# HGRN recurrence: eight heads written out as one pipeline in a fixed order, with an eighth of the reciprocals

## The chip, the cores and the metric

The kernel runs on one core of one Trainium2 chip. The metric is the device time of one execution in microseconds (us); lower is better. Times shown for the kernel before are three runs and one profiled execution.

## The reference, cut to what matters

The kernel computes two transformer-like blocks on a 512 x 1024 input. The change touches one part of the first block: the bidirectional HGRN2 scan over 8 heads, each with 128 key and 128 value channels, on 512 latent tokens after 256 context tokens.

```python
def _hgrn_scan(q, k, v, logf, S):      # S_t = diag(f_t) S_{t-1} + k_t v_t^T, o_t = S_t^T q_t
    L = H_CHUNK
    ...
        b = jnp.cumsum(lf, axis=2)
        attn = jnp.einsum('bhtd,bhtsd,bhsd->bhts', qc, decay, kc)
        o = jnp.einsum('bhtd,bhdv->bhtv', qc * jnp.exp(b), S) + jnp.einsum('bhts,bhsv->bhtv', attn, vc)
        S_new = jnp.exp(b_last)[..., None] * S + jnp.einsum('bhsd,bhsv->bhdv', kc * jnp.exp(b_last[:, :, None, :] - b), vc)
    ...
def _hgrn_gates(f_pre, lb):
    logf = jnp.log(lb + (1.0 - lb) * jax.nn.sigmoid(fp))
    k = (1.0 - lb) * jax.nn.sigmoid(-fp)
```

It is run once forwards and once backwards in time, and the two outputs are added. Gates f, keys k and queries q come from projections of the normed input by 1024 x 128 weight blocks, one block per head for q, for the forward gate and for the backward gate.

## The kernel before

The program is written in a tile framework: the source emits instructions for TensorE (PE), VectorE (DVE), ScalarE (ACT) and GpSimd (POOL), and a scheduler that plays the program through in advance chooses the order in which each engine's queue gets them. Buffers have tags with a number of slots; an instruction that wants a slot waits until its last user is done.

The stage in question is `block1_hgrn` (L981 on). Tokens are cut into 64 blocks of 8. For a head, `hgrn_head` makes q from one projection; `hgrn_dir`, called for both directions d, makes the gates F and the keys K from a second (512 latent columns) and a third (256 context columns) projection, and from them products of gates inside each block of 8: G (running products outwards from the middle of the block), R, the reciprocals of all 512 elements of G (L840), and the scaled queries Q1 and keys K1. Then `pre` and `suf` hold, for each of four levels, the products over the blocks that lie before and after a block inside a pair, a quad and so on (the loop at L862 to L873, run for each direction), and E holds the decays of the context (a scan, L882 and L885).

Products on TensorE: Y1, Y2 (inside a block, L907), then four levels (L910 to L926) in which both directions are put into one QM and one KM tile and multiplied into the PSUM banks X and Z; transposes of E and of KL (L953, L957), copied by ACT into kt; pk (L961, L963), the state increments, which S (L967, DVE) chains up; and po (L972 to L974), the output.

A projection (`proj`, `mm3`) is 24 matmuls on a weight block split into a high and a low part: `split_w` has ACT write the high part (L203) and DVE the low part (L204). Every weight block takes one such pair. The PSUM tags are `a` (four banks: X, Z, Y1, Y2 of a head, later pk of each direction), `p` (two, projections) and `t` (two, transposes and po). One `hgrn_head` after another is emitted, and the scheduler is free to lay the next head's projections and gates between the products of this one.

Of the kernel before, what the change touches and what calls it, by code (L numbers as in the profile page):

```python
# [8 lines left out]
F32 = mybir.dt.float32  # L9
# [5 lines left out]
ALU = mybir.AluOpType  # L15
# [3 lines left out]
KT = 8  # L19
# [123 lines left out]
class Net:  # L143
# [654 lines left out]
    def hgrn_dir(self, h, d, q):  # L798

        nc, w = self.nc, self.wk  # L800
        j = (self.HFF if d == 0 else self.HFB) + h
        wt = self.mix_w(j)
        F = w.tile([128, TA], F32, tag="w3", bufs=3, name=self.nm("F"))
        K = w.tile([128, TA], F32, tag="w3", bufs=3, name=self.nm("K"))
        bc = j - 4 + 4
        for seg, o, wd in (("x", 0, T), ("c", T, TC)):
            ps = self.proj(wt, seg)
            for t, b, sc in ((F, self.v("b_mix"), 1.0), (K, self.nbm, -1.0)):
                if seg == "x":
                    ov, iv = t[:, :T].rearrange("p (w r) -> p r w", r=8), ps.rearrange("p (r w) -> p r w", r=8)  # L810
                else:
                    ov, iv = t[:, T:], ps
                nc.scalar.activation(ov, iv, AF.Sigmoid, bias=b[:, j : j + 1], scale=sc)  # L813
        c = d * 8 + h
        nc.vector.tensor_scalar(F, F, self.omlb[:, c : c + 1], self.lb[:, c : c + 1], ALU.mult, ALU.add)
        f = F[:, :T].rearrange("p (b e) -> p b e", e=8)
        G = w.tile([128, 64, 9], F32, tag="w9", bufs=1, name=self.nm("G"))

        def two(t, i0, i1):

            st = i1 - i0
            return t[:, :, i0 : (i1 + (1 if st > 0 else -1)) if (st > 0 or i1 > 0) else None : st]

        mu = lambda o, a, b: nc.vector.tensor_tensor(o, a, b, ALU.mult)
        if d == 0:
            mu(two(G, 1, 5), two(f, 2, 4), two(f, 3, 5))
            mu(two(G, 0, 6), two(G, 1, 5), two(f, 1, 6))
            mu(two(G, 7, 8), two(G, 6, 0), two(f, 7, 0))
            nc.vector.tensor_copy(two(G, 2, 4), two(f, 3, 4))
            nc.gpsimd.memset(G[:, :, 3:4], 1.0)  # L830
            tL, tR = G[:, :, 8], G[:, :, 7]
        else:
            mu(two(G, 2, 6), two(f, 2, 4), two(f, 3, 5))
            mu(two(G, 1, 7), two(G, 2, 6), two(f, 1, 6))
            mu(two(G, 0, 8), two(G, 1, 7), two(f, 0, 7))
            nc.vector.tensor_copy(two(G, 3, 5), two(f, 3, 4))
            nc.gpsimd.memset(G[:, :, 4:5], 1.0)
            tL, tR = G[:, :, 0], G[:, :, 8]
        R = w.tile([128, 64, 8], F32, tag="w2", bufs=16, name=self.nm("R"))
        nc.vector.reciprocal(R, G[:, :, 0:8])  # L840
        Q1 = w.tile([128, 64, 8], F32, tag="w2", bufs=16, name=self.nm("Q1"))
        K1 = w.tile([128, 64, 8], F32, tag="w2", bufs=16, name=self.nm("K1"))
        kx = K[:, :T].rearrange("p (b e) -> p b e", e=8)
        qx = q.rearrange("p (b e) -> p b e", e=8)
        lo, hi = slice(0, 4), slice(4, 8)
        qg, qr = (hi, lo) if d == 0 else (lo, hi)
        om = self.omlb[:, c : c + 1]
        nc.vector.scalar_tensor_tensor(Q1[:, :, qg], qx[:, :, qg], om, G[:, :, qg], ALU.mult, ALU.mult)
        nc.vector.scalar_tensor_tensor(Q1[:, :, qr], qx[:, :, qr], om, R[:, :, qr], ALU.mult, ALU.mult)
        nc.gpsimd.tensor_tensor(K1[:, :, qr], kx[:, :, qr], G[:, :, qr], ALU.mult)  # L850
        nc.gpsimd.tensor_tensor(K1[:, :, qg], kx[:, :, qg], R[:, :, qg], ALU.mult)

        pre = w.tile([128, 5, 64], F32, tag="wp", bufs=4, name=self.nm("pre"))
        suf = w.tile([128, 5, 64], F32, tag="wp", bufs=4, name=self.nm("suf"))
        nc.vector.tensor_copy(pre[:, 0], tL)
        nc.vector.tensor_copy(suf[:, 0], tR)
        tots = w.tile([128, 128], F32, tag="wt", name=self.nm("tots"))
        o = 0
        n = 64
        mu(tots[:, 0:64], tL, tR)  # L860
        cur = tots[:, 0:64]
        for lv in range(4):  # L862
            m = 1 << lv
            pv = lambda t, i: t[:, i].rearrange("p (n two m) -> p n two m", two=2, m=m)
            tv = cur.rearrange("p (n two) -> p n two", two=2)
            nn = 64 // (2 * m)
            mu(pv(pre, lv + 1)[:, :, 1], pv(pre, lv)[:, :, 1], tv[:, :, 0:1].broadcast_to([128, nn, m]))
            nc.vector.tensor_copy(pv(pre, lv + 1)[:, :, 0], pv(pre, lv)[:, :, 0])
            mu(pv(suf, lv + 1)[:, :, 0], pv(suf, lv)[:, :, 0], tv[:, :, 1:2].broadcast_to([128, nn, m]))
            nc.vector.tensor_copy(pv(suf, lv + 1)[:, :, 1], pv(suf, lv)[:, :, 1])  # L870
            o += n
            n //= 2
            mu(tots[:, o : o + n], tv[:, :, 0], tv[:, :, 1])  # L873
            cur = tots[:, o : o + n]
        T128 = cur

        Fc, Kc = F[:, T:], K[:, T:]
        E = w.tile([128, TC], F32, tag="w1", bufs=1, name=self.nm("E"))
# [8 lines left out]
        return Q1, K1, pre, suf, T128, E  # L887

    def hgrn_head(self, h, v):
        nc, w = self.nc, self.wk  # L890
        wq = self.mix_w(self.HQ + h)
        ps = self.proj(wq, "x")
        bq = self.v("b_mix")[:, self.HQ + h : self.HQ + h + 1]
        sg = w.tile([128, T], F32, tag="w2", bufs=16, name=self.nm("sg"))
        nc.scalar.activation(sg, ps, AF.Sigmoid, bias=bq)
        q = w.tile([128, T], F32, tag="w2", bufs=16, name=self.nm("q"))
        nc.vector.scalar_tensor_tensor(q.rearrange("p (w r) -> p r w", r=8), ps.rearrange("p (r w) -> p r w", r=8), bq,
                                       sg.rearrange("p (r w) -> p r w", r=8), ALU.add, ALU.mult)
        D2 = [self.hgrn_dir(h, d, q) for d in range(2)]
        bc = lambda a, m: a.unsqueeze(a.ndim if hasattr(a, "ndim") else len(a.shape)).broadcast_to(list(a.shape) + [m])  # L900
        mm = nc.tensor.matmul
        X, Z, Y1, Y2 = [self.bank("a") for _ in range(4)]
        flat = [[D2[d][i].rearrange("p b e -> p (b e)") for i in range(2)] for d in range(2)]
        for Y, (qf, kf) in ((Y1, flat[0]), (Y2, flat[1])):
            for c in range(4):
                cs = slice(c * 128, c * 128 + 128)
                mm(Y[:, cs], kf[:, cs], qf[:, cs], start=True, stop=True)  # L907

        (Qf, Kf, pf, sf, _, _), (Qb, Kb, pb, sb, _, _) = D2
        for lv, dst, hb in ((3, X, 128), (2, X, 64), (1, X, 32), (0, Z, 128)):  # L910
            m = 1 << lv
            bv = lambda t: t.rearrange("p (n two m) e -> p n two m e", two=2, m=m)
            pv = lambda t: t[:, lv].rearrange("p (n two m) -> p n two m", two=2, m=m)
            QM = w.tile([128, 64, 8], F32, tag="w2", bufs=16, name=self.nm("QM"))
            KM = w.tile([128, 64, 8], F32, tag="w2", bufs=16, name=self.nm("KM"))
            for (o, a, p, i, e) in ((QM, Qf, pf, 1, nc.vector), (QM, Qb, sb, 0, nc.vector),
                                    (KM, Kf, sf, 0, nc.gpsimd), (KM, Kb, pb, 1, nc.gpsimd)):
                if m == 1:
                    e.tensor_tensor(bv(o)[:, :, i, 0], bv(a)[:, :, i, 0], bc(pv(p)[:, :, i, 0], 8), ALU.mult)
                else:  # L920
                    e.tensor_tensor(bv(o)[:, :, i], bv(a)[:, :, i], bc(pv(p)[:, :, i], 8), ALU.mult)
            qm, km = QM.rearrange("p b e -> p (b e)"), KM.rearrange("p b e -> p (b e)")
            for c in range(4):
                for b in range(128 // hb):
                    bs = slice(c * 128 + b * hb, c * 128 + b * hb + hb)
                    mm(dst[b * hb : b * hb + hb, bs], km[:, bs], qm[:, bs], start=True, stop=True)  # L926
# [1150 lines left out]
```

## Time and profile before

| what | value |
| --- | --- |
| three runs, median | 2606.16 us (2605.35 to 2611.03) |
| profiled execution, its own time | 2607.22 us |
| span of the profiled execution | 2605.4 us |
| TensorE busy in the span | 2512.9 us (96%) |
| VectorE busy in the span | 1651.4 us (63%) |

Busy time of TensorE is made of modelled ends, so a share of 96% says that its queue was rarely empty and not that it ran at its peak. The shares are means over stages that have different limits; the stage of the change is about 319 us of the span.

### The profile page before, as it was taken

To read this page: it belongs to the slowest core of one execution; us is meant where nothing else is said; L and a number is where in the kernel's file an instruction comes from. 1 tells how busy PE (TensorE), PEld (TensorE's weight loads), DVE (VectorE), ACT (ScalarE), POOL (GpSimd) and SP (SyncE) were. 2 spreads that over 40 slices of the span, in tenths; PEclk is the share of its full clock that TensorE was granted. 3 is DMA by queue.
4 is the path that set the end of the run, shared out by engine and by line. 5 is a ranking of instruction groups with operands and counts; after the bars stand their busy time and mean duration, and the time that the engine had idled before them with its cause. 6 is when DMAs were issued, how large, how long until landed. Compare 5 with 4: busy or idle time off the path is not lost. (4 is left out here: it accounts for less than half of the span.)

```text
span 2605.4 us, 38102 instructions
## 1 busy us (share of the span) xinstructions
PE 2512.9 (96%) x15116; PEld 2157.3 (83%) x15116; DVE 1651.4 (63%) x3087; ACT 965.1 (37%) x1711; POOL 452.2 (17%) x567
## 2 busy tenths in 40 slices
PE   6999999999989998999999999999999899999998
PEld 4888888899988888898888898888886668888887
DVE  8777767746499996324433366665555777766665
ACT  5312211236233332425422363232343556533333
POOL 3000000012043344214000011062013440100001
PEclk8999999999999999999999999999999999999999
DMA  6434664621211111111333342344423223333332
GB/s 230 174 125 145 230 216 178 226 90 66 85 41 50 33 50 41 37 49 41 89 121 97 96 139 89 117 127 154 137 72 112 64 77 99 109 97 96 97 97 72
DMA packets 88307, 277.94 MB, mean 107 GB/s; under 512 B 12912, under 2 KB 31104, under 8 KB 79936
## 3 DMA queue, kind: packets, MB, share of 16 engines
q1 hardware_dynamic: 85344, 265.00, 31.7%
q0 software_dynamic: 2064, 7.35, 0.8%
q10 hardware_dynamic: 720, 3.15, 0.3%
q8 instruction: 119, 1.95, 0.3%
q14 instruction: 60, 0.49, 0.1%
HBM read 262.88 MB, written 12.59 MB: 106 GB/s over the span
## 5 line engine op out<-in xcount | busy, mean ns | idle before, releaser
L204 DVE TENSOR_TENSOR wlo<-wraw,whi 128x1024 fp32r<-128x1024 f32 (+1 forms) x341 | 423.2, 1246 | 235.2 <-ACT whi L203 105.0
L203 ACT ACTIVATE whi<-wraw 128x1024 fp32r<-128x1024 f32 (+1 forms) x341 | 355.4, 1053 | 553.7 <-PE psa L216 158.1
L215 PE MATMUL psp<-xmh,whi 128*128 128x512 f32 (+1 forms) x760 | 281.1, 377 | 3.7 <-ACT K L813 3.1
L216 PE MATMUL psp<-xml,whi 128*128 128x512 f32 (+1 forms) x744 | 272.4, 373 | 0.0
L350 POOL TENSOR_TENSOR ssum<-ssum,sq 128x256 f32<-128x256 f32 x40 | 30.2, 754 | 962.0 <-ACT sq L348 961.5
L215 PE MATMUL psa<-xmh,whi 128*128 128x512 f32 x496 | 194.0, 391 | 0.0
L216 PE MATMUL psa<-xml,whi 128*128 128x512 f32 x496 | 193.9, 391 | 0.0
L215 PE MATMUL psu<-xmh,whi 128*128 128x512 f32 x496 | 193.5, 390 | 0.0
L216 PE MATMUL psu<-xml,whi 128*128 128x512 f32 x496 | 193.3, 390 | 0.0
L215 PE MATMUL pso<-hh,whi 128*128 128x512 f32 (+1 forms) x512 | 184.3, 365 | 1.8 <-DVE hr L496 1.8
L216 PE MATMUL pso<-hl,whi 128*128 128x512 f32 (+1 forms) x512 | 184.2, 365 | 0.0
L215 PEld LDWEIGHTS psp<-xmh,whi 128*128 128x128 f32 x760 | 148.5, 195 | 29.0 <-ACT K L813 4.7
L305 DVE SCALAR_TENSOR_TENSOR ajunk<-araw,crow 128x1024 bf16<-128x1024 f32 x128 | 156.4, 1222 | 25.2 <-DMA araw<-in_ada_r_dram 19.6
L218 PE MATMUL psp<-xmh,wlo 128*128 128x512 f32 (+1 forms) x744 | 170.3, 368 | 0.0
L492 DVE SCALAR_TENSOR_TENSOR xr<-pso,hgate,xr 128x512 f32<-128x512 f32 x128 | 95.3, 749 | 109.8 <-PE pso L218 109.7
L216 PEld LDWEIGHTS psp<-xml,whi 128*128 128x128 f32 x744 | 145.1, 195 | 22.1 <-issue 0.6
L218 PEld LDWEIGHTS psp<-xmh,wlo 128*128 128x128 f32 x744 | 129.3, 189 | 26.3 <-issue 4.4
L218 PE MATMUL pso<-hh,wlo 128*128 128x512 f32 (+1 forms) x512 | 145.2, 365 | 0.0
L218 PE MATMUL psa<-xmh,wlo 128*128 128x512 f32 x496 | 126.8, 389 | 0.0
L218 PE MATMUL psu<-xmh,wlo 128*128 128x512 f32 x496 | 124.0, 390 | 0.0
L215 PEld LDWEIGHTS pso<-hh,whi 128*128 128x128 f32 x512 | 97.2, 190 | 16.5 <-DVE hr L496 2.0
L444 ACT ACTIVATE hh<-sa 128x512 fp32r<-128x512 f32 x66 | 36.7, 560 | 197.1 <-DVE sa L441 197.0
(667 smaller groups left out, 5818.1 us busy)
## 6 DMA issues: line engine op xcount, KB each, us to landing
araw<-in_ada_r_dram SPq DMA_DIRECT2D x52, 1024.0 KB, 5.5
wraw<-in_ffn_in_dram SPq DMA_DIRECT2D x88, 512.0 KB, 4.3
wraw<-in_mix_fm_dram SPq DMA_DIRECT2D x65, 512.0 KB, 3.6
wraw<-in_ffn_out_dram SPq DMA_DIRECT2D x44, 512.0 KB, 3.7
wraw<-in_up_dram SPq DMA_DIRECT2D x44, 512.0 KB, 3.7
wraw<-in_down_dram SPq DMA_DIRECT2D x22, 512.0 KB, 3.7
araw<-in_ada_w_dram SPq DMA_DIRECT2D x8, 1024.0 KB, 11.7
wraw<-in_mix_out_dram SPq DMA_DIRECT2D x14, 512.0 KB, 3.7
```

The lines of the kernel that those rows point to most:

```text
L203: nc.scalar.activation(hi, raw, AF.Copy)
L204: nc.vector.tensor_tensor(lo, raw, hi.bitcast(F32), ALU.subtract)
L215: self.nc.tensor.matmul(ps, wh, xh, start=k == 0, stop=False)
L216: self.nc.tensor.matmul(ps, *((wl, xh) if last else (wh, xl)), start=False, stop=False)
L218: self.nc.tensor.matmul(ps, *((wh, xl) if last else (wl, xh)), start=False, stop=k == n - 1)
L305: nc.vector.scalar_tensor_tensor(junk, w[:, h], 1.0, cr[:, n], ALU.mult, ALU.mult, accum_out=o[:, k : k + 1])
L350: (eng or nc.vector).tensor_tensor(acc, acc, t, ALU.add)
L444: nc.scalar.activation(hh, sa, AF.Copy)
L492: self.anchor = nc.vector.scalar_tensor_tensor(res[n], p, gt[:, n : n + 1], res[n], ALU.mult, ALU.add)
```

## The change

`hgrn_dir` and `hgrn_head` go; `hgrn_pipe` writes all eight heads out inside `tc.manual_schedule(engines={PE, DVE, Activation, Pool})`. Inside that region each of the four engines takes its instructions in the order in which the source emits them; the SP queue (weight loads) and where other stages' instructions fall between stay the scheduler's. Parts:

- gates: the products G go straight into rows of one tile `hgx`, and both a product and its reciprocal partner are laid out so that one reciprocal of 128 elements per direction does, the others following by multiplication with f. Of DVE's three small copies per head and direction, two become ACT copies (one in `hgx`, one into PS0) and one is folded into a product; the scaling of the latent F goes to ACT too.
- block products: one tile holds before/after and both directions, so that a level is one multiplication, one copy and one total for all four.
- order in one turn of the loop for head h, with n = h+1: first projection of n; Q1; levels 3 and 2; Y1, Y2; second projection of n; levels 1 and 0; QL, KL; forward gates of n; transposes; both context projections of n; split of the next weight block; backward gates of n; the copies that free X, Z, Y1, Y2; block products of n; pk; context scan of n; q projection of n; split; S; po; split; output copies.

```diff
+    def hgrn_gates(self, h, d, F, K, PS0):
...
+            nc.scalar.activation(at(q_ + 3, k_ + 5), f(3, 4), AF.Copy)
+            mu(at(q_ + 2, k_ + 6), f(2, 4), f(3, 5))
+            mu(at(q_ + 1, k_ + 7), at(q_ + 2, k_ + 6), f(1, 6))
+            mu(one(q_ + 0), one(q_ + 1), f(0))
+            mu(PS0[:, 1, d], one(k_ + 7), f(7))
+            nc.scalar.activation(PS0[:, 0, d], one(q_ + 0), AF.Copy)
+            nc.vector.reciprocal(at(k_ + 0, q_ + 7), at(q_ + 0, k_ + 7))
...
-        R = w.tile([128, 64, 8], F32, tag="w2", bufs=16, name=self.nm("R"))
-        nc.vector.reciprocal(R, G[:, :, 0:8])
...
+    def hgrn_pipe(self, v):
...
+        for h in range(8):
+            n = h + 1
+            more = n < 8
+            if more:
+                fx = [self.hgrn_fx(n, 0, wt[0])]
+                PS0, K1n = ps0(), []
+            Q1 = self.hgrn_q1(h, *pq)
+            X, Z, Y1, Y2 = [self.bank("a") for _ in range(4)]
+            self.hgrn_level(3, X, 128, Q1, K1, lev)
+            self.hgrn_level(2, X, 64, Q1, K1, lev)
...
+            if more:
+                fx.append(self.hgrn_fx(n, 1, wt[1]))
+            self.hgrn_level(1, X, 32, Q1, K1, lev)
+            self.hgrn_level(0, Z, 128, Q1, K1, lev)
...
+            if more:
+                K1n.append(self.hgrn_gates(n, 0, *fx[0], PS0))
+            kts = []
+            for d in range(2):
...
+                nc.scalar.activation(kt[:, 0:2], pt[:, :256].rearrange("p (c t) -> p c t", c=2), AF.Copy)
...
+            if more:
+                fc = [self.hgrn_fc(n, d, wt[d]) for d in range(2)]
+                wq = wt[2]
+            if n < 7:
+                raw = self.hgrn_w(n + 1)
+                wt = [self.hgrn_split(raw[0])]
+            if more:
+                K1n.append(self.hgrn_gates(n, 1, *fx[1], PS0))
...
+            nc.scalar.activation(at, X, AF.Copy)
+            nc.vector.copy_predicated(v4(at), m4(self.m8), v4(Z))
...
+            T128 = ends
+            if more:
+                lev, ends = self.hgrn_blocks(PS0)
+            pks, S = [], []
+            for d in range(2):
+                pk = self.bank("a", [128, 4, 128])
...
+            if more:
+                E = [self.hgrn_ctx(n, d, *fc[d]) for d in range(2)]
+                pq = self.hgrn_q(n, self.proj(wq, "x"))
+            if n < 7:
+                wt.append(self.hgrn_split(raw[1]))
+            for i in range(3):
+                for d in range(2):
...
+                    nc.vector.scalar_tensor_tensor(S[d][:, i + 1], S[d][:, i], T128[:, 4 * d + c : 4 * d + c + 1], pks[d][:, i + 1],
+                                                   ALU.mult, ALU.add)
+            po = self.bank("o", [128, 4, 128])
...
+            if n < 7:
+                wt.append(self.hgrn_split(raw[2]))
...
+                with tc.manual_schedule(engines={e.PE, e.DVE, e.Activation, e.Pool}):
+                    self.hgrn_pipe(v)
```

## Rows read from the trace of the kernel before

**Rows 1.** Page, busy us of each engine (share of the span) x instructions.
```profile
PE 2512.9 (96%) x15116; PEld 2157.3 (83%) x15116; DVE 1651.4 (63%) x3087; ACT 965.1 (37%) x1711; POOL 452.2 (17%) x567
```

**Rows 2.** Windows: stretch, length, busy us by engine, granted clock, DMA share, GB/s.
```profile
698.80:1018.10 319.30, 291.38 (x2075) 259.91 (x2074) 286.63 (x710) 108.69 (x218) 121.12 (x172) 0.95 0.15 46
879.50:917.20 37.70, 35.13 (x257) 31.46 (x256) 35.05 (x89) 13.46 (x28) 15.30 (x22) 0.95 0.15 42
1000.10:1018.10 18.00, 12.60 (x120) 11.60 (x121) 12.11 (x39) 1.81 (x5) 5.28 (x11) 0.81 0.01 2
```

**Rows 3.** Waits, 720 to 1000 us: who for whom, total, times, longest.
```profile
PE psa L907 <- DVE pre L868: 17.9, 7, 4.3
```

**Rows 4.** Timeline of TensorE in one head: start, length, instructions.
```profile
880.07 1.06 PE L907 MATMUL psa<-Q,K 128*128 128x128 f32 x8
892.97 3.07 PEld L926 LDWEIGHTS psa<-QM,KM 128*128 128x128 f32 x64
905.44 0.38 PE L215 MATMUL psp<-xmh,whi 128*128 128x256 f32 x1 [0.44 <-ACT K L813]
908.42 0.40 PE L215 MATMUL psp<-xmh,whi 128*128 128x512 f32 x1
913.89 0.39 PE L215 MATMUL psp<-xmh,whi 128*128 128x512 f32 x1
991.10 0.39 PE L972 MATMUL pso<-v,at 128*128 128x128 f32 x2
991.32 0.39 PE L973 MATMUL pso<-st,QL 128*128 128x128 f32 x2
```

**Rows 5.** Groups of ACT by shape, 760 to 1000 us: busy, mean ns.
```profile
L813 ACT ACTIVATE F<-psp,vec 128x512 f32<-128x512 f32 x12 | 14.3, 1189 | 26.3 <-PE psp L218 17.2 <-POOL G L830 9.2
L813 ACT ACTIVATE K<-psp,nbm 128x512 f32<-128x512 f32 x12 | 13.7, 1144 | 0.0
L813 ACT ACTIVATE F<-psp,vec 128x256 f32<-128x256 f32 x12 | 5.6, 469 | 0.0
L954 ACT ACTIVATE kt<-pst 128x256 f32<-128x256 f32 x12 | 4.6, 386 | 0.0
L965 ACT ACTIVATE st<-psa 128x128 f32<-128x128 f32 x12 | 3.6, 300 | 30.7 <-PE psa L963 30.7
L939 ACT ACTIVATE at<-psa 128x512 f32<-128x512 f32 x6 | 3.6, 598 | 6.9 <-PE psa L926 6.9
```

**Rows 6.** Groups of DVE by shape, 760 to 1000 us.
```profile
L840 DVE RECIPROCAL R<-G 128x512 f32<-128x512 f32 x13 | 43.4, 3341 | 0.7
L824 DVE TENSOR_TENSOR G<-F 128x128 f32<-128x128 f32 x13 | 5.2, 396 | 0.2
L824 DVE TENSOR_TENSOR pre<-pre,tots 128x32 f32<-128x32 f32 x48 | 8.9, 185 | 0.2
L824 DVE TENSOR_TENSOR tots<-G 128x64 f32<-128x64 f32 x13 | 3.6, 276 | 0.2
```

**Rows 7.** Timeline of ACT and DVE: a weight split, six state steps, mLSTM's first operation.
```profile
892.33 1.06 ACT L203 ACTIVATE whi<-wraw 128x1024 fp32r<-128x1024 f32 x1 [4.78 <-PE psp L216]
893.58 1.21 DVE L204 TENSOR_TENSOR wlo<-wraw,whi 128x1024 fp32r<-128x1024 f32 x1
1013.58 2.12 DVE L967 SCALAR_TENSOR_TENSOR st<-st,tots,psa 128x128 f32<-128x128 f32 x6
1015.81 0.74 DVE L1124 TENSOR_SCALAR mq<-psp,vec 128x512 f32<-128x512 f32 x1
```

**Rows 8.** Windows of one us around two waits of TensorE (columns as in rows 2).
```profile
887.00:888.00 1.00, 0.33 (x1) 0.36 (x2) 1.00 (x8) 0.54 (x2) 0.12 (x1) 0.85 0.00 0
891.00:892.00 1.00, 1.00 (x9) 1.00 (x9) 1.00 (x6) 0.00 (x0) 0.39 (x1) 0.95 0.00 0
1003.00:1004.00 1.00, 0.00 (x0) 0.00 (x0) 1.00 (x7) 0.00 (x0) 0.37 (x2) 0.87 0.00 0
1005.00:1006.00 1.00, 0.98 (x4) 1.00 (x5) 0.94 (x3) 0.00 (x0) 0.88 (x1) 0.50 0.00 0
1010.00:1011.00 1.00, 1.00 (x9) 1.00 (x8) 0.18 (x1) 0.00 (x0) 0.00 (x0) 0.71 0.00 0
```

More of the change, by code (lines that the diff above doesn't have):

```diff
@@ new lines, in hgrn_w, with hgrn_split, w2, hgrn_fx @@
+    def hgrn_w(self, h):
+        return [self.load_w(self.ins["mix_fm"][j + h], [KT, 128]) for j in (self.HFF, self.HFB, self.HQ)]
+    def hgrn_split(self, raw):
+        h, l = self.split_w(raw, [KT, 128])
+        return [(h[:, k], l[:, k]) for k in range(KT)]
+    def w2(self, name):
+        return self.wk.tile([128, 64, 8], F32, tag="w2", bufs=17, name=self.nm(name))
+    def hgrn_fx(self, h, d, wt):
+        nc = self.nc
+        j, c = (self.HFF, self.HFB)[d] + h, d * 8 + h
+        ps = self.proj(wt, "x")
+        F, K = self.w2("F"), self.w2("K")
+        for t, b, sc in ((F, self.v("b_mix"), 1.0), (K, self.nbm, -1.0)):
+            nc.scalar.activation(t.rearrange("p w r -> p r w"), ps.rearrange("p (r w) -> p r w", r=8), AF.Sigmoid,
+                                 bias=b[:, j : j + 1], scale=sc)
+            if t is F:
+                nc.scalar.activation(F, F, AF.Identity, scale=self.omlb[:, c : c + 1], bias=self.lb[:, c : c + 1])
+        return F, K
@@ new lines, in hgrn_q, with hgrn_q1 @@
+    def hgrn_q(self, h, ps):
+        nc = self.nc
+        bq = self.v("b_mix")[:, self.HQ + h : self.HQ + h + 1]
+        sg, q = self.w2("sg"), self.w2("q")
+        p8 = ps.rearrange("p (r w) -> p r w", r=8)
+        nc.scalar.activation(sg.rearrange("p w r -> p r w"), p8, AF.Sigmoid, bias=bq)
+        return sg, q, bq, p8
+    def hgrn_q1(self, h, sg, q, bq, p8):
+        nc = self.nc
+        pm = lambda t: t.rearrange("p w r -> p r w")
+        nc.vector.scalar_tensor_tensor(pm(q), p8, bq, pm(sg), ALU.add, ALU.mult)
+        out = []
+        for d in range(2):
+            t = self.w2("Q1")
+            c = d * 8 + h
+            nc.vector.scalar_tensor_tensor(t, q, self.omlb[:, c : c + 1],
+                                           self.hgx[:, 2 * d].rearrange("p (b e) -> p b e", e=8), ALU.mult, ALU.mult)
+            out.append(t)
+        return out
@@ new lines, in hgrn_level @@
+    def hgrn_level(self, lv, dst, hb, Q1, K1, lev):
+        nc = self.nc
+        m = 1 << lv
+        bv = lambda t: t.rearrange("p (n two m) e -> p n two m e", two=2, m=m)
+        pv = lambda s, d: lev[lv][:, s, d].rearrange("p (n two m) -> p n two m", two=2, m=m)
+        QM, KM = self.w2("QM"), self.w2("KM")
+        for (o, a, p, i, e) in ((QM, Q1[0], pv(0, 0), 1, nc.vector), (QM, Q1[1], pv(1, 1), 0, nc.vector),
+                                (KM, K1[0], pv(1, 0), 0, nc.gpsimd), (KM, K1[1], pv(0, 1), 1, nc.gpsimd)):
+            if m == 1:
+                x = p[:, :, i, 0]
+                e.tensor_tensor(bv(o)[:, :, i, 0], bv(a)[:, :, i, 0], x.unsqueeze(2).broadcast_to([128, 32, 8]), ALU.mult)
+            else:
+                x = p[:, :, i]
+                e.tensor_tensor(bv(o)[:, :, i], bv(a)[:, :, i], x.unsqueeze(3).broadcast_to([128, 32 // m, m, 8]), ALU.mult)
+        qm, km = QM.rearrange("p b e -> p (b e)"), KM.rearrange("p b e -> p (b e)")
+        for c in range(4):
+            for b in range(128 // hb):
+                bs = slice(c * 128 + b * hb, c * 128 + b * hb + hb)
+                nc.tensor.matmul(dst[b * hb : b * hb + hb, bs], km[:, bs], qm[:, bs], start=True, stop=True)
@@ L905, in hgrn_head @@
             for c in range(4):
                 cs = slice(c * 128, c * 128 + 128)
[L907 to L922, printed above, removed]
-            for c in range(4):
-                for b in range(128 // hb):
-                    bs = slice(c * 128 + b * hb, c * 128 + b * hb + hb)
-                    mm(dst[b * hb : b * hb + hb, bs], km[:, bs], qm[:, bs], start=True, stop=True)
@@ L969, in hgrn_head @@
-        po = self.bank("o", [128, 4, 128])
-        for c in range(4):
-            cs = slice(c * 128, c * 128 + 128)
-            mm(po[:, c], at[:, cs], v[c][:, h], start=True, stop=False)
-            mm(po[:, c], QE[0][:, cs], S[0][:, c], start=False, stop=False)
-            mm(po[:, c], QE[1][:, cs], S[1][:, 3 - c], start=False, stop=True)
-        o = self.hp.tile([128, 4, 128], F32, tag="tok", name=self.nm("hh"))
-        for c in range(4):
-            nc.scalar.activation(o[:, c], po[:, c], AF.Square, accum_out=self.ssh[:, c, h : h + 1])
@@ L978, in hgrn_head @@
-        nc.scalar.activation(o, po, AF.Copy)
-        return o
+                mm(po[:, c], at[:, cs], v[c][:, h], start=True, stop=False)
+                mm(po[:, c], QE[0][:, cs], S[0][:, c], start=False, stop=False)
+                mm(po[:, c], QE[1][:, cs], S[1][:, 3 - c], start=False, stop=True)
+            if n < 7:
+                wt.append(self.hgrn_split(raw[2]))
+            o = self.hp.tile([128, 4, 128], F32, tag="tok", name=self.nm("hh"))
+            for c in range(4):
+                nc.scalar.activation(o[:, c], po[:, c], AF.Square, accum_out=self.ssh[:, c, h : h + 1])
@@ L981, in block1_hgrn @@
+            nc.scalar.activation(o, po, AF.Copy)
+            self.hh.append(o)
+            if more:
+                K1 = K1n
     def block1_hgrn(self):
@@ L986, in block1_hgrn @@
             with self.pool(name="wk", bufs=2) as self.wk:
-                self.hh = [self.hgrn_head(h, v) for h in range(8)]
+                self.hh = []
+                self.hgx = self.xp.tile([128, 8, 512], F32, tag="xr", name="hgx")
+                e = mybir.EngineType
+                with tc.manual_schedule(engines={e.PE, e.DVE, e.Activation, e.Pool}):
+                    self.hgrn_pipe(v)
     def mlstm_rows(self, rp):
```

243 lines of the change are left out of this document (117 added, 126 removed).

## Prediction

> **What bounds the kernel now.** I read the page first: TensorE is busy in 96% of the span [rows 1], so any gain has to come from stretches in which it waits or runs slowly. The windows put the HGRN stage at 698.8 to 1018.1 us, 319.3 us long [rows 2]. In it DVE is busy for 286.6 us, and in one head of 37.7 us (879.5 to 917.2) for 35.05. There DVE comes closest to being full. TensorE is busy for 35.1 of the 37.7 at a mean clock of 0.95. The waits view names the price: its products Y wait for DVE's block products, 17.9 us in 7 heads, 2.5 a head [rows 3]. Each such wait also lowers the clock: after the one that ends at 887.7 the granted clock stands at half (1.2 GHz) from about 887.8 to 891.05 [rows 8].
>
> TensorE's own work in a head at full clock follows from the timeline [rows 4]. A latent projection takes 913.89 - 908.42 = 5.47 us, a context one 908.42 - 905.44 = 2.98, the levels 3.07, four of the eight Y products 1.06 in eight passes, so 0.12 a pass of full width (a plain fp32 matmul shows as two passes, a transpose as one), and po's passes start 0.11 apart. So 3 x 5.47 + 2 x 2.98 + 3.07 + 2 x 0.97 (eight starts of 0.12) + ten transposes 1.2 + 20 passes of pk 2.5 + 24 passes of po 2.65 = 33.7 us. The change leaves every matmul in place. Before, 33.7 + 2.5 of waiting + 1.5 lost to the half clock make 37.7. A perfect pipeline gains 4 us a head.
>
> **The change part by part.** *DVE's work.* Two reciprocals of 512 elements at 3.34 us become two of 128; between 3.34 and nothing, in proportion 0.84 each: 5.0 us saved a head. The block products were 42 operations at 0.17 to 0.35 us plus four copies; 13 are left, four of 128 elements at 0.40 as those of G, four copies and five totals of 0.15 to 0.28 [rows 6]: about 6 us saved. The scaling of the latent F moves to ACT. DVE is left with 23 to 26 us a head. It is no longer the bound, and the 2.5 us wait for it disappears.
>
> *The fixed order.* Four queues now go strictly in the order written, so each instruction is held by whatever the one ahead of it waits for. I walked through one turn (with a next head) on these durations, 0.1 to 0.2 us for each hand-over (892.33 + 1.06 to 893.58 is 0.19 [rows 7]). Three places stop TensorE.
>
> First wait, transposes. The second direction's transposes need the two `t` banks back, so ACT's two kt copies. On ACT they stand behind the second projection's work: two sigmoids of 1.19 and 1.14, the scaling of F (512 wide, taken as the `at` copy, 0.60) and two small gate copies of 0.30 at most [rows 5]. That is 3.5 us after the projection ends, then a copy of 0.39 and a hand-over: 4.0. TensorE meanwhile has levels 1 and 0 (1.4) and one direction's transposes (0.6). Wait: 2.0 us, up to 3.0 when the gate products on DVE, which write the same rows of `hgx` as the copy, are held for it.
>
> Second wait, pk. It needs a free `a` bank, and the first to come free is X, by ACT's `at` copy. Before that copy ACT has, in the order written: the second context projection's sigmoids (2 x 0.47, not before that projection ends), the high part of the next weight block (1.06), the gate copies of the backward direction. The second of these needs three DVE products (0.40 + 0.40 + 0.28, some 0.8 overlapped), and DVE stands in front of them at the low part of the same weight block (1.21), which waits for the high part. So from the end of the context projection: 0.94 + 1.06 + 1.21 + 0.8 + 0.3 + 0.60 (`at`) + five hand-overs 0.7 = 5.6 us without work for TensorE. What stands behind pk: the q projection and po. The second pk waits some 0.3 more for DVE's first masked copy.
>
> Third wait, po. It needs all six state steps, 2.12 us in a row [rows 7]. DVE has the low part of another weight block ahead of them, ACT the sigmoid of q ahead of its high part, and that needs the q projection: 1.17 (now a permuted write, taken as F's 1.19) + 1.06 + 1.21 + 2.12 + 0.5 of hand-overs = 6.1 us after the projection, less the first products of po, 0.2: 5.9.
>
> Together 2.0 + 5.9 + 5.9 = 13.8 us at full clock, 47.5 a head. POOL isn't in it: its products stay the same but for K1, made in one piece instead of two, and it is busy for 15.3 us of a head now [rows 2]; the first of them need only the turn before. Weight loads aren't either: a block's slot is free a head before.
>
> *The clock.* TensorE idles three times a head for 2 to 6 us. The trace has two such waits. The 2.1 us one cost 3.2 us of half clock, 1.6 of work. The one of 3.2 us before 1005 cost more: the clock is at half from 1003.9 to 1010.3, of which 5.3 us were work, 2.65 lost [rows 8]. So three waits cost 4.8 to 8.0; I take 1.7 each, nearer the lower end, as projections of full width stand behind two of the three: 52.6 a head.
>
> *The sum.* Head 0 is prepared alone: three latent and two context projections, 22.4 us, then a wait for the sigmoid of q and the next weight block (3.8, with clock 5.5): 28. From there to the end of the first turn's context projections 3.6 + 5.47 + 5.47 + 1.4 + 3.2 + 5.96 and 1.7 of clock make 27: 55. Six turns of 52.6: 371. The seventh turn's rest splits fewer blocks: waits 3.3 and 1, work 10.8, clock 1.7: 388. The last head has nothing beside it, as now: 18.0 us from 1000.1 to 1018.1 [rows 2]: 406. About 2 us of it can run under the stage before. So 404 against 319.3, **+85**. From the profiled execution's 2607.2 this gives 2692; its own time lies 1.1 above the median, so **2691 us**.
>
> Bounds. With no clock loss beyond today's and the short first wait a head is 47.5 (6.5 turns fewer by 5.1, prologue and end by 4: +48). With 2.65 a wait and the long first wait it is 56.5: +112.
>
> **A rule that speaks for the change, and one against.** DVE's 35.05 busy us in a head of 37.7 are the row [rows 2]. The Trainium skill, Perfetto Trace Analysis, section Identifying the Most-Contended Engine, says to optimize first the engine with the highest occupancy. By that rule the head shrinks to the next engine's work, which is the first rival's time. Against it stands the Trainium skill, TensorE: Matmul & The Clock Gate, section Architectural detail (the array is 16× 32×32): VectorE and ScalarE queues are strictly first in, first out, and TensorE's can only pull weight loads ahead. By this one the three waits stay whole, as summed.
>
> **The rivals.** *Faster: the heads run at TensorE's pace.* Then 22.4 + 7 x 33.7 + 18.0 = 276, 43 less: **2563 us**. For it: DVE's excess is gone, and every operation in the turn has a head's length of other work beside it. Against: the ACT and DVE instructions that hold X and S stand after the projections they wait for, in both queues. It decides at about 39.5 a head (85 / 6.5 = 13 under 52.6): if all waits with their clock come to less than 6 us, the kernel isn't slower.
>
> *Waits partly filled.* Other stages' instructions may still fall between. In the old trace the mLSTM stage's first projection ran inside this one: DVE takes its result at 1015.8, before po is through [rows 7]. If two of its projections filled waits in each of the last three turns (33 us moved, clock kept), or one of the long waits were missing in every turn (7.6 x 6.5 = 49), the time would be **2640 to 2658 us**. Against: three weight slots, and the HGRN blocks come first.
>
> *The change frees DVE but nothing of it shows* (waits as long as the old ones): within 5 us of **2606 us**.
>
> *More waits than I see*, through rows of `hgx` shared by three engines or slots of `w2`: 5 us more in each turn, **2725 us**.
>
> **How the numbers follow.** Forecast and its bounds (2654 to 2718): 0.62. Partly filled below 2654: 0.12. Faster: 0.16. Unchanged: 0.05. Above 2718: 0.05. The likeliest is 2691, with its own range 2654 to 2718. The range for 8 in 10 goes down through the partly filled case and the unchanged one to 2600, and up to 2722: outside it are nearly all of the faster case and the tail above. A measurement here tells 0.2%, 5.2 us, from no change: faster 0.16, same 0.04, slower 0.80.
>
> **What would show it.** In the new trace: turns of 47 to 56 us between first projections; TensorE idle before the first pk, named after ACT's `at`; idle before po's second product, named after DVE's state steps; idle before the third group of transposes, named after ACT's kt copies; each followed by a granted clock of 0.5; DVE busy under 60% of the turn; reciprocals near 0.9 us. I am wrong if ACT's `at` copy ends within 2 us of the context projection's end, or if the state steps follow pk at once. Then the sum goes to the first rival.

## The result, and the profile after

The kernel after takes 2699.79 us (median of 4 runs, 2698.25 to 2702.2), the kernel before in the same comparison 2605.94: a ratio of 1.0357, 95% interval 1.0339 to 1.0374. It is slower by 94 us, where 85 were forecast.

The page after, engine line and granted clock by slices (answers to [rows 1]):

```profile
PE 2540.4 (94%) x15116; PEld 2177.0 (81%) x15116; DVE 1592.2 (59%) x2855; ACT 997.0 (37%) x1760; POOL 461.4 (17%) x539
...
PEclk8999999999988888999999999999999998999999
```

The matmuls are the same 15116. DVE has 59 us less to do, and the program is slower all the same. The run of five 8s in the clock line is the stage of the change. Windows of the stage, of one turn (from one first pk to the next) and of the last head, and of single microseconds around the three waits of a turn (columns as in [rows 2]):

```profile
698.50:1103.50 405.00, 317.51 (x2076) 279.09 (x2075) 226.31 (x478) 139.41 (x266) 130.65 (x142) 0.88 0.12 36
862.51:913.64 51.13, 38.80 (x255) 34.30 (x255) 26.66 (x60) 17.25 (x34) 16.41 (x17) 0.87 0.10 31
1080.50:1103.50 23.00, 20.59 (x176) 18.05 (x176) 14.48 (x25) 5.49 (x17) 7.53 (x13) 1.00 0.12 38
901.00:902.00 1.00, 0.16 (x1) 0.17 (x2) 0.80 (x3) 0.80 (x3) 0.00 (x0) 1.00 0.00 0
902.00:903.00 1.00, 0.97 (x8) 0.76 (x8) 0.93 (x3) 0.68 (x3) 0.00 (x0) 1.00 0.00 0
910.00:911.00 1.00, 0.00 (x0) 0.00 (x0) 0.57 (x1) 0.73 (x2) 0.00 (x0) 0.83 0.00 0
917.00:918.00 1.00, 1.00 (x8) 1.00 (x8) 1.00 (x3) 0.00 (x0) 0.00 (x0) 0.75 0.00 0
927.00:928.00 1.00, 0.00 (x0) 0.00 (x0) 1.00 (x5) 0.00 (x0) 1.00 (x3) 0.87 0.44 33
928.00:929.00 1.00, 0.55 (x2) 0.55 (x3) 1.00 (x3) 0.00 (x0) 0.51 (x1) 0.50 0.56 209
934.00:935.00 1.00, 1.00 (x4) 0.78 (x4) 1.00 (x4) 0.87 (x4) 1.00 (x1) 0.72 0.00 0
```

The stage is 405.0 us long, and 319.3 before [rows 2]. A turn takes 51.13 us, and DVE is busy for 52% of it. What TensorE waits for in the stage (answers to [rows 3]):

```profile
PE psa L1048 <- ACT at L1035: 33.9, 8, 5.1
PE pso L1070 <- DVE st L1063: 27.1, 6, 4.6
PE pst L1017 <- ACT kt L1018: 19.1, 7, 2.7
```

The old wait of Y [rows 3] is gone, and three new ones stand there: pk for ACT's `at` copy, po for the state steps, the transposes for ACT's kt copy. One turn in TensorE's timeline, in its order:

```profile
901.84 0.44 PE L1017 MATMUL pst<-ident,E 128*128 128x128 f32 x2 [2.74 <-ACT kt L1018]
...
913.64 1.22 PE L1048 MATMUL psa<-v,kt 128*128 128x128 f32 x4 [5.06 <-ACT at L1035]
...
928.45 0.80 PE L1070 MATMUL pso<-st,QL 128*128 128x128 f32 x2 [4.49 <-DVE st L1063]
```

How the second of these comes about, in the timeline of ACT and DVE:

```profile
908.61 0.47 ACT L832 ACTIVATE fc<-psp,vec 128x256 f32<-128x256 f32 x1 [2.04 <-PE psp L218]
908.99 0.47 ACT L832 ACTIVATE fc<-psp,nbm 128x256 f32<-128x256 f32 x1
909.34 1.05 ACT L203 ACTIVATE whi<-wraw 128x1024 fp32r<-128x1024 f32 x1
...
910.43 1.23 DVE L204 TENSOR_TENSOR wlo<-wraw,whi 128x1024 fp32r<-128x1024 f32 x1 [6.74 <-ACT whi L203]
911.57 0.38 DVE L852 TENSOR_TENSOR hgx<-F 128x128 f32<-128x128 f32 x1
912.05 0.70 DVE L852 TENSOR_TENSOR hgx<-hgx,F 128x128 f32<-128x128 f32 x2
...
912.78 0.32 ACT L870 ACTIVATE ps<-hgx 128x64 f32<-128x64 f32 x1 [2.06 <-DVE hgx L852]
913.00 0.58 ACT L1035 ACTIVATE at<-psa 128x512 f32<-128x512 f32 x1
```

From the second line on, each is held by one above it, by its queue or its data. X, which the `at` copy reads, was complete before all this: its last products stand ahead of both directions' transposes, of which the second begin at 901.84. The copy is late by its place in ACT's queue. DVE stands idle for 6.74 us ahead of the low part of the weight block, then ACT for 2.06 us ahead of a copy of 64 elements that needs three DVE products.

The third wait has the same form (timeline again):

```profile
923.55 1.19 ACT L926 ACTIVATE sg<-psp,vec 128x512 f32<-128x512 f32 x1 [5.19 <-PE psp L218]
...
924.52 2.00 ACT L203 ACTIVATE whi<-wraw 128x1024 fp32r<-128x1024 f32 x2
925.62 1.23 DVE L204 TENSOR_TENSOR wlo<-wraw,whi 128x1024 fp32r<-128x1024 f32 x1 [1.33 <-ACT whi L203]
926.76 1.63 DVE L1063 SCALAR_TENSOR_TENSOR st<-st,tots,psa 128x128 f32<-128x128 f32 x6
```

Groups by shape, 760 to 1060 us (answers to [rows 5, 6]): the scaling of F measured 0.81 us (0.60 estimated), the reciprocals 0.96 (0.84 estimated), and the first of DVE's gate products on `hgx` is held by ACT's scaling.

```profile
L822 ACT ACTIVATE F<-F,lbc,omlb 128x512 f32<-128x512 f32 x12 | 9.8, 814 | 0.4
...
L860 DVE RECIPROCAL hgx<-hgx 128x128 f32<-128x128 f32 x6 | 5.7, 956 | 1.2 <-ACT ps L859 1.2
...
L852 DVE TENSOR_TENSOR hgx<-F 128x128 f32<-128x128 f32 x12 | 4.7, 393 | 32.6 <-ACT F L822 32.6
```

### The profile page after: what moved, and what is told of

Its sections match the earlier page's. It is cut to its first block, busy times and chain, and to the rows that moved or that the text cites. A ratio compares the mean times of both kernels' runs of the same rounds, so it can differ in the third digit from the quotient of the medians.

```text
span 2696.5 us, 37860 instructions
## 1 busy us (share of the span) xinstructions
PE 2540.4 (94%) x15116; PEld 2177.0 (81%) x15116; DVE 1592.2 (59%) x2855; ACT 997.0 (37%) x1760; POOL 461.4 (17%) x539
## 5 line engine op out<-in xcount | busy, mean ns | idle before, releaser
L305 DVE SCALAR_TENSOR_TENSOR ajunk<-araw,crow 128x1024 bf16<-128x1024 f32 x128 | 156.2, 1221 | 26.1 <-DMA araw<-in_ada_r_dram 19.1
```

What stands on the lines that cost most here:

```text
L305: nc.vector.scalar_tensor_tensor(junk, w[:, h], 1.0, cr[:, n], ALU.mult, ALU.mult, accum_out=o[:, k : k + 1])
```

## The experiments

My theory: the three queue waits and the clock that they cost make the whole loss, and come from the places that the order gives to a few ACT and DVE instructions. Rivals: a fixed order loses as such; the new parts themselves are slower; a wait taken away comes back elsewhere. Medians below are over 4 or 5 runs; "before" ran beside them at 2607 to 2608 us.

**The scheduler's own order.** Everything of the change but the fixed order:

```diff
-                with tc.manual_schedule(engines={e.PE, e.DVE, e.Activation, e.Pool}):
-                    self.hgrn_pipe(v)
+                self.hgrn_pipe(v)
```

> The changed kernel without the region that fixes the order: the same operations and buffers, the scheduler picks the order. Theory: the rewriting took 10 us or so a head from DVE and the order alone costs the time, so this is no slower than the kernel before: 2575 to 2608 us. Rival A: the rewriting is what costs, so it stays above 2650. Rival B says nothing of this one beyond a gain.

Measured: 2587.05 us, ratio to before 0.9917 (0.9901 to 0.9934). Of the three waits only the one for the state steps is left, at 1.4 us or less:

```profile
PE pso L1070 <- DVE st L1063: 9.9, 8, 1.4
PE psa L961 <- DVE QM L956: 3.5, 7, 0.7
```

So the rewritten source gains 21 us, and the written order costs 113.

**Single moves.** Three kernels each take away one of the waits. First the copies that free X, Z, Y1, Y2 (`at` and DVE's four masked copies), put ahead of the context projections:

```diff
+            nc.scalar.activation(at, X, AF.Copy)
...
             if more:
                 fc = [self.hgrn_fc(n, d, wt[d]) for d in range(2)]
...
-            nc.scalar.activation(at, X, AF.Copy)
```

> Only the copies that free X, Z, Y1 and Y2 (ACT's at copy, DVE's four masked copies, GpSimd's sum) are written ahead of the context projections; everything else stays. Theory (the written order makes the waits): the wait before pk, 33.9 us in all eight turns, falls to under 6 us, and with it 1.6 to 2.65 us of half clock in each of seven turns: 35 to 50 us less than the changed kernel, 2650 to 2665 us. Rival A (the rewritten gates and block products themselves are slow, on ACT and DVE): within 5 us of 2700. Rival B (one chain of ACT and DVE carries the turn, so a wait that is taken away comes back at the next place): the po wait grows by as much, gain under 10 us, 2690 to 2700.

Measured: 2666.14 us, 1.0221 (1.0205 to 1.0238): 34 us faster, 1 us less than expected. The pk wait is gone (1.1 us left in one turn), but part of it came back at po:

```profile
PE pso L1070 <- DVE st L1063: 45.1, 6, 7.5
```

The po wait went from 27.1 to 45.1, over half of what was taken away. DVE's gate products, block products and state steps still stand behind the same weight split, while TensorE is there sooner. Second, the split of the second weight block behind the state steps:

```diff
-            if n < 7:
-                wt.append(self.hgrn_split(raw[1]))
             for i in range(3):
...
+            if n < 7:
+                wt.append(self.hgrn_split(raw[1]))
             po = self.bank("o", [128, 4, 128])
```

> Only the split of the second weight block is written behind the state steps instead of ahead of them. Theory: the state steps no longer stand behind the sigmoid of q and a weight block, so the wait before po, 27.1 us in six turns, goes to under 5 us, with 1.6 to 2.65 us of half clock each: 32 to 40 us less, 2660 to 2668 us. Rival A: within 5 us of 2700. Rival B: the split comes later, the next turn's second projection or DVE's Q1 waits for it instead, gain under 10 us.

Measured: 2673.24 us, 1.0253 (1.0238 to 1.0268), 5 us short of the expectation. The po wait fell from 27.1 to 10.5, but the wait for QM at the levels rose from 2.8 to 9.1. Third, the second projection behind the transposes:

```diff
-            if more:
-                fx.append(self.hgrn_fx(n, 1, wt[1]))
             self.hgrn_level(1, X, 32, Q1, K1, lev)
...
+            if more:
+                fx.append(self.hgrn_fx(n, 1, wt[1]))
             if more:
                 fc = [self.hgrn_fc(n, d, wt[d]) for d in range(2)]
```

> Only the next head's second gate projection is written behind the transposes instead of ahead of the levels 1 and 0. Theory: ACT's kt copies no longer stand behind that projection's sigmoids, so the wait before the second direction's transposes, 19.1 us in seven turns, goes to under 7 us; with the clock 20 to 30 us less, 2670 to 2680 us; if the forward gates' small copies still hold ACT, only 10. The levels 1 and 0 may wait some for DVE, as their products come 5.5 us earlier. Rival A: within 5 us of 2700. Rival B: the second gates come later, the pk wait grows by 2 us or more a turn, gain under 10 us.

Measured: 2681.0 us, 1.0279 (1.0258 to 1.03). The transposes' 19.1 us of waiting are gone and the time is 18.8 us shorter, 1 us less than expected (the profiled execution, 2684.14, is 14.1 shorter). Other waits grew by some 8 us: QM from 2.8 to 5.9, the projections for ACT's K from 0.5 to 3.3, po from 27.1 to 29.1. So this sum doesn't tell what clock the wait cost; the rows of the kernel after do, with a granted clock of 1.00 from 901 to 903.

**One link of the chain.** The split of the first block moved behind the copies:

```diff
-            if n < 7:
-                raw = self.hgrn_w(n + 1)
-                wt = [self.hgrn_split(raw[0])]
             if more:
                 K1n.append(self.hgrn_gates(n, 1, *fx[1], PS0))
...
             nc.gpsimd.tensor_tensor(at, at, self.dg, ALU.add)
+            if n < 7:
+                raw = self.hgrn_w(n + 1)
+                wt = [self.hgrn_split(raw[0])]
```

> One term of the second wait alone: the split of the next head's first weight block is written behind the copies that free the banks instead of ahead of the backward gates. Theory (the wait before pk is a sum of what stands ahead of ACT's at copy): it loses ACT's 1.06 us and DVE's 1.21 us and one or two hand-overs, so it falls from about 5.06 to about 2.6 us in six turns, 15 us in all. The clock still falls, so 14 to 17 us less than the changed kernel: 2683 to 2686 us. Rival (the at copy is held by the context sigmoids or the gate products only, and the split runs beside them): the wait stays at 5, time within 4 us of 2700.

Measured: 2683.09 us, 1.0287 (1.0272 to 1.0303). The wait lost 14 us of its 33.9, as the sum of its links said:

```profile
PE psa L1048 <- ACT at L1032: 19.7, 7, 2.9
```

**All three single moves together** (the diffs of the three moves under "Single moves", at once).

> The three moves of the first three runs together. If the waits were independent, their gains of 34, 27 and 19 us would add up to 80: 2620 us. Theory: with the copies early, DVE still has the weight split, the backward gates, the block products and the context scans ahead of the state steps, some 13 us after the context projections against 8 for pk and the q projection, so a wait of about 5 us before po stays in each of six turns; the other two go. 2610 to 2630 us. Rival B (one chain, a wait taken away comes back): above 2640.

Measured: 2644.58 us, 1.0144 (1.0127 to 1.0161). This missed by 15 us and more and lies where rival B put it: the three waits aren't three separate sums. With the copies early and the transposes free, TensorE comes to po 40.4 us too soon in all:

```profile
PE pso L1070 <- DVE st L1061: 40.4, 7, 6.4
```

DVE's timeline of this kernel shows what is ahead of the steps: DVE works without a pause from the split to their end.

```profile
882.18 1.23 DVE L204 TENSOR_TENSOR wlo<-wraw,whi 128x1024 fp32r<-128x1024 f32 x1 [1.68 <-ACT whi L203]
...
886.99 0.28 DVE L898 TENSOR_TENSOR tots<-ps 128x128 f32<-128x128 f32 x1
...
892.20 1.09 DVE L890 TENSOR_TENSOR_SCAN E<-fc,zero 128x255 f32<-128x255 f32 x1
893.22 1.61 DVE L1061 SCALAR_TENSOR_TENSOR st<-st,tots,psa 128x128 f32<-128x128 f32 x6
```

Backward gates (883.33 to 886.99), block products (to 890.7) and the context's scans (to 893.2) of the *next* head all go ahead of this head's state steps. In the kernel after, DVE did most of this work while TensorE waited for pk and ran the q projection, and it held po up by nothing.

**Another fixed order.** The same instructions, in an order in which nothing that TensorE waits for soon stands behind the next head's work: copies and second projection between the two directions' transposes, context projections after them, state steps ahead of the scans and the q projection.

```diff
...
+            turn(0)
             at = flat(self.w2("at"))
...
+                fx.append(self.hgrn_fx(n, 1, wt[1]))
+            turn(1)
+            if more:
+                K1n.append(self.hgrn_gates(n, 1, *fx[1], PS0))
+            if more:
+                fc = [self.hgrn_fc(n, d, wt[d]) for d in range(2)]
...
-                E = [self.hgrn_ctx(n, d, *fc[d]) for d in range(2)]
-                pq = self.hgrn_q(n, self.proj(wq, "x"))
-            if n < 7:
-                wt.append(self.hgrn_split(raw[1]))
             for i in range(3):
...
+            if n < 7:
+                wt.append(self.hgrn_split(raw[1]))
+            if more:
+                E = [self.hgrn_ctx(n, d, *fc[d]) for d in range(2)]
+                pq = self.hgrn_q(n, self.proj(wq, "x"))
```

`turn(d)` holds one direction's transposes and kt copies. The split of the third block goes behind level 0 of the next turn.

> The same operations in another fixed order: the copies of X directly behind the first direction's transposes, the second projection between the two directions' transposes, the backward gates ahead of the context projections, the state steps ahead of the context scans and of the second split, the third split a turn later behind Q1. By the walk over the queues every wait before pk and po is covered. Theory: 35 to 37 us a turn, at or below the free order's 2587: 2575 to 2595 us. Rival (a fixed order as such costs, against one the scheduler picks): above 2610.

Measured: 2587.81 us, 0.9923 (0.9908 to 0.9938), the time of the scheduler's own order. So a fixed order as such need not cost anything.

**The clock.** To tell the waits' length from the clock that they cost, unread matmuls of full width fill the two long waits: 20 ahead of pk, 18 ahead of po, on the weight block of q. They change no result.

```diff
+            if more:
+                dm = self.bank("p")
+                for i in range(20):
+                    (wh, wl), (xh, xl) = wq[i % 8], self.xm[i % 8]
+                    mm(dm, wh, xh, start=i == 0, stop=i == 19)
             for d in range(2):
                 pk = self.bank("a", [128, 4, 128])
...
```

> What the clock adds to the waits. The changed kernel with matmuls that nobody reads put into the waits before pk (20 of 512 columns, some 4.6 us) and before po (18, some 4.1 us) in seven turns: about 61 us more work on TensorE, nothing taken away. Theory (each wait also costs 1.6 to 2.65 us of half clock behind it): the fill runs inside the waits, the clock stays up, and 13 waits give back 20 to 34 us less the bit by which the fill is late, 5 us at most: 2668 to 2685 us. Rival (the waits alone make the time, no clock term): 2697 to 2705 us. If the fill delays what comes behind it: up to 2760.

Measured: 2676.19 us, 1.0262 (1.0247 to 1.0278). Some 61 us more work for TensorE (7 x 38 x 0.23), and 24 us less time. The waits for `at` and the state steps, 61.0 before, are down to 13.1:

```profile
PE psa L1053 <- DVE at L1036: 5.6, 6, 0.9
PE pso L1080 <- DVE st L1068: 4.3, 7, 1.1
PE psa L1053 <- ACT at L1035: 3.2, 6, 0.5
```

Work and rest of the waits make 13 us more than the waits did. So some 37 us came from the clock, a little over 5 in each of seven turns. The rows of the kernel after say the same: half clock from 910.66 (slice of 0.83) to 917.5 (0.75), of which 3.86 us are work after the second wait, and from 927.74 to 934.56, of which 6.11 are; half of both lost makes 5.0. Windows of 90 us inside the stage, kernel after and then this one, show the clock itself, 0.85 and 1.00:

```profile
860.00:950.00 90.00, 70.67 (x454) 62.28 (x455) 49.73 (x111) 28.09 (x55) 31.52 (x33) 0.85 0.11 36
```

```profile
860.00:950.00 90.00, 81.94 (x562) 70.62 (x561) 55.25 (x108) 33.84 (x65) 28.14 (x33) 1.00 0.09 30
```

**Where the rewritten source's 21 us come from.** Two kernels put work back on DVE, in the scheduler's order. The first adds one reciprocal of 384 unread elements per direction and head:

```diff
+        junk = self.w2("R")
+        nc.vector.reciprocal(junk[:, :48], C[:, 0].rearrange("p (b e) -> p b e", e=8)[:, :48])
```

> The kernel after in the scheduler's own order, plus one reciprocal of 384 elements for each direction and head whose result nobody reads: DVE gets back the 2.5 us per direction and head that the few reciprocals had taken from it, about 40 us over the eight heads, and nothing else changes. Theory that the fewer reciprocals are what makes the rewritten kernel faster (DVE was the fullest engine): the time goes from 2587 back up by 8 to 21 us, to 2595 to 2608, and waits of TensorE for DVE appear. Rival: DVE has slack for it and the gain lies elsewhere (block products, copies moved to ACT): within 4 us of 2587.

Measured: 2583.95 us, 0.9909 (0.9895 to 0.9922): my theory fell, the rival holds. The windows from 700 to 1000 us, before and with the old reciprocals:

```profile
700.00:1000.00 300.00, 277.59 (x1949) 247.32 (x1947) 273.22 (x671) 106.59 (x212) 115.85 (x161) 0.95 0.16 49
```

```profile
700.00:1000.00 300.00, 289.61 (x2129) 255.47 (x2128) 270.49 (x499) 139.93 (x281) 126.10 (x153) 0.99 0.17 50
```

DVE is as full as before (270.5 against 273.2 us of 300) and TensorE does 12 us more in the same stretch. Nothing waits for the unread reciprocals, so this tests how much DVE has to do, and not how long the chain of products is that TensorE waits for. The second makes the block products twice:

```diff
+                self.hgrn_blocks(PS0)
                 lev, ends = self.hgrn_blocks(PS0)
```

> The kernel after in the scheduler's own order, with the block products made twice in each head and one of the two sets left unread: some 3.7 us more work on DVE in each head, about 30 us in all, in one piece that stands ahead of the levels. If DVE's amount of work sets the time: up by 6 to 15 us, 2593 to 2602. If DVE has slack: within 4 us of 2587. If what counts is how late the block products are (a latency), more than 15 us: over 2602.

Measured: 2591.72 us, 0.9934 (0.992 to 0.9948), 4.7 above the scheduler's own order and between the two bounds: a small price at most. Then the sequence: all of the next head's work emitted behind the head, in the scheduler's order.

```diff
...
             if more:
-                K1 = K1n
+                PS0, K1 = ps0(), []
+                for d in range(2):
+                    K1.append(self.hgrn_gates(n, d, *self.hgrn_fx(n, d, wt[d]), PS0))
+                fc = [self.hgrn_fc(n, d, wt[d]) for d in range(2)]
+                pq = self.hgrn_q(n, self.proj(wt[2], "x"))
+                lev, ends = self.hgrn_blocks(PS0)
+                E = [self.hgrn_ctx(n, d, *fc[d]) for d in range(2)]
+            if n < 7:
+                raw = self.hgrn_w(n + 1)
+                wt = [self.hgrn_split(r) for r in raw]
```

> The kernel after in the scheduler's own order, and with the source written head by head as before: all of the next head's projections, gates, block products, scans and weight splits are emitted behind the output copies of the head, in the sequence in which head 0 is prepared. Gates, block tile, few reciprocals and copies stay as in the kernel after. More work on VectorE was shown not to matter (2584 with the old amount of reciprocals), so two causes are left for the 20 us by which the new parts beat the kernel before. Theory: it is the sequence of emission, from which the scheduler gets a next head's gates earlier: 2600 to 2612 us, and the wait of Y or of the levels for the block products comes back (15 to 25 us). Rival: it is the parts themselves (a shorter chain from the sigmoids to K1 and the block products, and fewer big buffers that a direction waits for): within 6 us of 2587, and no such wait.

Measured: 2619.45 us, 1.0048 (1.0034 to 1.0061). The time goes up by 32 us, more than expected, so the sequence of the source matters to the new parts: one po to the next takes 39.8 us in most turns, against 35.9 in the scheduler's order without this edit and 37.7 before. The wait of Y doesn't come back, as the theory had it; others come, 34.9 us in four kinds, the largest

```profile
PE psp L215 <- DVE q L932: 13.5, 8, 2.1
PE psa L961 <- DVE QM L956: 8.9, 8, 1.9
```

The sequence here is that of head 0, which isn't quite the one of the kernel before, and no kernel has the old parts in the new sequence. So how the 21 us divide between the parts and the sequence stays open; the amount of DVE's work makes a few of them at most (3 us less and 5 us more in the two kernels above).

**A further step, which failed.** Y1 and Y2 ahead of level 3 in the reordered kernel:

```diff
+            for Y, d in ((Y1, 0), (Y2, 1)):
...
             self.hgrn_level(3, X, 128, Q1, K1, lev)
             self.hgrn_level(2, X, 64, Q1, K1, lev)
-            for Y, d in ((Y1, 0), (Y2, 1)):
...
```

> The reordered kernel with one more move: the products Y1 and Y2, which need only Q1 and K1, stand ahead of level 3 instead of behind level 2, so that TensorE has 2 us of work while DVE and POOL write QM and KM of level 3. My theory: the waits for QM (14.1 us in 22 in the reordered kernel) shrink to under 6 us and the time falls by 5 to 14 us, to 2573 to 2583 us. Rival: DVE and POOL make the levels one after another at their own pace, so the wait only moves to a later level: sum of the QM waits unchanged, 2585 to 2590 us.

Measured: 2597.95 us, 0.996 (0.9947 to 0.9972), 10 us slower than without the move. The rival was right that the wait only moves; it also gathers in one place. Reordered kernel, then this one:

```profile
PE psa L961 <- DVE QM L956: 7.5, 15, 1.3
PE psa L961 <- DVE QM L953: 6.6, 7, 0.9
```

```profile
PE psa L961 <- DVE QM L953: 14.0, 8, 2.0
PE psa L961 <- DVE QM L956: 3.9, 10, 0.9
```

3.8 us more of waiting alone don't make 10 us. In windows of one us from 855 to 935 the reordered kernel never leaves the full clock; here it is at half from 880 to 883.4 and from 917.6 to 921, behind waits of 1.98 and 1.97 us at level 0. The first slice:

```profile
880.00:881.00 1.00, 1.00 (x7) 1.00 (x6) 1.00 (x2) 0.00 (x0) 0.00 (x0) 0.50 0.00 0
```

## Why the prediction was right, point by point

- **The place and the cause of the three waits**: right. Each stands where the walk through the turn put it, under the same names, and the moves show the causes: when what holds it is moved, the wait for the transposes goes, that for pk goes but for 1.1 us, and that for po falls from 27.1 to 10.5. By the Trainium skill, TensorE: Matmul & The Clock Gate, section Architectural detail (the array is 16× 32×32), ACT's and DVE's queues are strictly first in, first out. The trace agrees, with the `at` copy at 913.00 behind the gate copy that waited 2.06 us.
- **Their sizes**: transposes 2.74 (2.0 to 3.0; it was the long case, with DVE held for ACT's copy into `hgx`), pk 5.06 (5.6 and 0.3 for a second wait that didn't come), po 4.49 (5.9). The third term was over-sized most: six state steps took 1.63 us, not 2.12, and the hand-overs, put at 0.5, took nothing, as each row starts when the one before it ends or a little earlier.
- **The clock**: 5.0 us a turn against 5.1, right in the sum and wrong in its parts. I gave each of three waits 1.7. Measured are nothing after the transposes, 1.9 after pk's wait and 3.05 after po's. The price came from slices read a little short: where a slice holds both levels, the share at half is twice what its mean lacks to 1.00. By [rows 8] the clock was at half from 887.7 to 891.1, and from 1003.74 to 1010.58, of which 5.6 us were work, 2.8 lost (3.2 us at half, and 2.65 lost, in the prediction). "Each such wait also lowers the clock" didn't hold for the transposes.
- **A turn**: 33.7 + 2.74 + 5.06 + 4.49 + 5.0 = 51.0; measured 51.13, forecast 52.6. Six turns are 8.7 us less than summed.
- **The rest of the stage** made up for it. The prologue up to the first pk wait took 56.7 (55), the seventh turn's rest 18.4 (17), and the last head 23.0, not 18.0 "with nothing beside it": two projections of the next stage, 11 us of work, ran between its products (in the kernel before, the stage held the same two earlier on). The 2 us that I let run under the stage before were 0.3. Together 405.0 for 404: the errors cancelled, so that the sum comes out within 1 us is luck.
- **What was missed**: the program behind the stage took 1593.0 us after and 1587.3 before, 5.7 of the 91 by which the two profiled executions differ. In the twelve kernels of the experiments it took 1584.3 to 1591.8. What sets these few us wasn't tried.
- **What bounds the kernel before**: this reading failed. I took DVE's 35.05 busy us in a head of 37.7 [rows 2] as the limit, and the wait for the block products as its sign. The profile names the block product L868, because it ended last before Y began, but Y reads only Q1 and K1. DVE and then TensorE in the timeline of the kernel before:

```profile
879.53 3.35 DVE L840 RECIPROCAL R<-G 128x512 f32<-128x512 f32 x1
...
884.66 1.53 DVE L921 TENSOR_TENSOR QM<-Q,pre 128x256 f32<-128x256 f32 x3
...
887.05 0.47 DVE L849 SCALAR_TENSOR_TENSOR Q<-q,omlb,R 128x256 f32<-128x256 f32 x1
...
887.67 2.03 PE L907 MATMUL psa<-Q,K 128*128 128x128 f32 x8 [2.13 <-DVE pre L868]
```

  L849 writes the second half of one direction's Q1; it ends at 887.52 and Y begins 0.15 us later, the same 0.15 in all eight heads. Its data R were there from 882.88, but the other direction's level products (QM, QL) stood ahead of it in DVE's queue. So Y waited for Q1, late by its place, and not for the block products. With DVE as full as that, but with the added work outside this chain, the kernel runs at 2584 and that wait isn't there; nor is it in the kernel written head by head, which points to the new parts and not to the sequence. By the Trainium skill, Perfetto Trace Analysis, section Identifying the Most-Contended Engine, one optimizes the engine with the highest occupancy first. In the rewritten kernel, in the scheduler's order, some 40 us less reciprocal work on DVE bought nothing (2587.05 without that work, 2583.95 with it).
- **The rival "at TensorE's pace"** named the right potential: one po to the next is 35.9 us in the scheduler's own order; with the old reciprocals it is 34.7 in four of six turns and 35.9 on the mean of the six; the work is 33.7. Its mechanism was there, and the fixed order kept it from showing.

## What to carry to other kernels

When an order is written out by hand, list for each instruction that frees a bank or feeds the next product what stands ahead of it in its own queue, and what that waits for: a copy of 0.6 us whose data were ready cost 5 us a turn, because a weight split and a handful of gate products of the next head stood in front. Waits of one turn share links, so their prices don't add: undo them together and look at which one comes last then (three moves that gave 79 us singly gave 55). A busy engine isn't a bound until more work on it makes the kernel slower; an experiment that adds unread work tells it in one run. And where a profile names what a wait ended on, look in the source whether the waiting instruction reads it.

## What was not expected of the hardware

A wait's length doesn't tell whether TensorE's clock falls. In the kernel after, the granted clock stayed at 1.00 through a wait of 2.74 us (901 to 903), and fell to half, 1.2 GHz, in those of 5.06 and 4.49. With Y1 and Y2 moved it fell after a wait of 1.98 us (with one of 0.27 ahead of it). Waits of 0.41, 0.45 and 0.94 us within 7 us, in the reordered kernel, left it whole. What TensorE did ahead of these waits differs, and which difference decides wasn't tried. Filling the waits with unread products pays for itself: 61 us more work, 24 us less time.
